# All S5 table rounds ahead of the quads, two quads' loads ahead for the second half, and the gelu and z stores issued by ScalarE

## The chip, the core and the metric

The kernel runs on one core of a Trainium2 chip. The metric is the device time of one execution in microseconds; the figure for the kernel before is the median of three runs, and one further execution was profiled. Engine names as in the profile: PE is TensorE, DVE is VectorE, ACT is ScalarE, POOL is GpSimd, SP is SyncE, which does no arithmetic here and issues every DMA of the kernel before. Each engine takes its own instructions strictly in the order in which they stand in its program.

## What is computed

One inference step of a hybrid decoder layer, all in float32, for a prompt of 2048 tokens and 8 single-token samples (2056 columns). The parts that matter here:

```
proj = rmsnorm(x) @ w_in              # 1024 -> 512 columns u (S5) + 512 columns v (pooling)
# S5 head: 32 groups x 16 channels, 64 complex states per group
h    = scan over time of (a_bar * h + b_bar u)
y    = gelu(Re(C h) + D u);   y = y * sigmoid(y @ w_glu)
# pooling head: 4 channel groups, windows 2/4/8/16
z    = (windowed mean(v) - v) @ pool_w * pool_scale
x    = x + concat(y, z) @ w_out
x    = x + w_down(gelu(conv(w_up rmsnorm(x)))...)   # gated FFN, 2 x 2816 wide
```

The FFN takes some 1400 of the 2000 us and is not touched by the change. What it touches is the mixer in front of it.

## The kernel before, in words

**Tiles and halves.** The columns are cut into five `SUBS` (512, 512, 512, 264 and 256 columns) and, from the gate on, into eight `CSUBS` of about 256. Time is also cut into two halves of 1024 tokens, since the S5 state of the second half starts from the end of the first. Weights are [128 x 128] blocks. Each float32 operand is split into a high and a low part (a cast on ACT, a subtraction on DVE or POOL: `split`, lines 75 and 76), and a product is three matmuls (`mm3`, lines 87 to 89).

**The input projection.** `units(half, ms, subs)` runs one `unit` for each column tile and each of eight blocks `m` of 128 outputs. For m = 0 to 3 the result is a piece of u: it is scaled by DVE (line 733) and stored to `u_d`. For m = 4 to 7 it is a piece of v: `pool_path` takes the windowed sums (DVE lines 657, 662, 673; POOL line 665 `wsum`) and `pool_z` multiplies by `pool_w` (PE line 697 into `ps_z`), lets ACT scale the result into `zt` (line 699; two buffers) and stores it to `z_d` in one or two DMAs (line 703). `prep_x` loads and splits the next column tile of x (`xraw`, `xh` on ACT line 79, `xl` on DVE line 80).

**The S5 part in the background.** The 32 groups are eight quads of four groups. Pieces of S5 work wait in the list `bg`; `back()` takes the next one after each unit and gives it a priority that lies 50 steps (`BGO`) behind the units, so that a scheduler lays it between them when engines are free. The pieces are:
- `rot(r)`, r = 0 to 3: a round that builds a quarter of the rotation table by doublings, 20 DVE instructions on `rt` with the scratch tile `ra` (`level`, lines 279, 280, 282), a copy and a negation on ACT (lines 290 and 295), and four stores to `tab_d[r]` by SP (lines 298 and 299). `rt` shares the two buffers of the tag `tab` with the quads' own tables, and `ra` shares the single buffer of the tag `yg` with the gelu's result.
- `s5_build(q)`: operators of quad q, mostly on POOL, with eight small DMAs `ops<-kt` (line 539).
- `s5_load(half, q)`: loads `U`, the operators (second half only) and `tab` (lines 552 to 566).
- `s5_scan(half, q)`: four matmuls into `psw` (line 585), the rotation and the scan on DVE (lines 600 to 613), the result `H` (line 619). `psw` has one buffer.
- `s5_out(half, q)`: eight matmuls into `psy` (lines 637 and 638), gelu on ACT into `yg` (line 639), and a store to `y_d` by SP (line 640).

The list for the first half is build 0, rot 0, build 1, rot 1, then for each quad: load, (for the first two quads) the next round, scan of the quad before, out of the quad before that. So rounds 2 and 3 stand between the loads and the first two scans.

**The transition.** When the list is empty, `s5_queue(1)` puts the second half's 24 pieces in it, and `units(1, (6, 7), [2])` and, after the load of `w_glu` (`wgr`, split into `wg0` to `wg3`) and of y (`y_load`, which needs all four `y_d[m]` of the first half), `units(1, (6, 7), [3, 4])` finish the projection. Then `gate_in` multiplies y by `w_glu` (`ps_g`), loads z back (`zr`), and `out_proj` multiplies with `w_out` (`wo0` to `wo7`, loaded through two raw buffers by `res_w`, line 859) into `ps_o`, calling `back()` once for each of the eight row blocks d. All of `bg` has to be done before the gate of column tile 4 (`s5_end`).

**DMA completion.** Each DMA signals on one of eight semaphores in rotation, whichever engine issues it, so an issue also waits until the DMA eight places before it has landed.

Of the kernel before, what the change touches and what calls it, by code (L numbers as in the profile page):

```python
# [40 lines left out]
BGO = 50  # L41
# [3 lines left out]
def build(tc, a):  # L45
    nc = tc.nc
    V, S, P, T, Y = nc.vector, nc.scalar, nc.gpsimd, nc.tensor, nc.sync
    es = ExitStack()
    with es:
# [3 lines left out]
        y_d = [[dram.tile([8, 128, 128], F32, name=f"y_d{m}_{h}") for h in range(2)] for m in range(4)]  # L53
# [121 lines left out]
        with ExitStack() as er_:  # L175
# [108 lines left out]
            def rot(r):  # L284


                cs = slice(4 * r, 4 * r + 4)
                tab = sp.tile([128, 2, 4, 128], F32, tag="tab", name="rt", bufs=2)
                ta = sp.tile([128, 2, 4, 64], F32, tag="yg", name="ra")
                S.copy(out=tab[:, :, :, 0:8], in_=pwr["tab0"][:, :, cs])  # L290
                for lv in range(3, 7):
                    n = 1 << lv
                    level(tab, ta[:, :, :, 0:n], lv, cs, tab[:, :, :, 0:n], tab[:, :, :, n:2 * n])
                neg = ta.rearrange("p x g c -> p (x g c)").rearrange("p (g c) -> p g c", c=128)
                S.mul(out=neg, in_=tab[:, 1], mul=-1.0)
                for gl in range(2):
                    gp = slice(gl * 64, gl * 64 + 64)
                    Y.dma_start(out=tab_d[r][:, 0:2, :, gl], in_=tab[gp].rearrange("n x (q e) c -> n x q e c", e=2))
                    Y.dma_start(out=tab_d[r][:, 2, :, gl], in_=neg[gp].rearrange("n (q e) c -> n q e c", e=2))
# [328 lines left out]
            def s5_out(half, qd):  # L628
                U, ops, tab, H = lds.pop((half, qd))
                m, r0 = qd // 2, (qd % 2) * 64  # L630
                n = 128 if half == 0 else 136
                o = 136 - n
                yg = sp.tile([128, 4, 136], F32, tag="yg", name="yg", bufs=1)
                yps = psW.tile([128, 4, 256], F32, tag="Yp", name="psy")
                for i in range(4):
                    yo = yps[:, i, 0:n]
                    T.matmul(yo, lhsT=ops[:, i, 128:256], rhs=U[:, i, o:136], start=True, stop=False)
                    T.matmul(yo, lhsT=ops[:, i, 272:400], rhs=H[:, i, o:136], start=False, stop=True)
                S.activation(out=yg[:, :, 0:n], in_=yps[:, :, 0:n], func=AF.Gelu)
                Y.dma_start(out=y_d[m][half][:, r0:r0 + 64].rearrange("t (h g) c -> t h g c", h=16), in_=yg[:, :, n - 128:n])  # L640
                if half == 1:
                    Y.dma_start(out=ys_d[m][r0:r0 + 64].rearrange("(h g) n -> h g n", h=16), in_=yg[0:16, :, 0:8])

# [50 lines left out]
            def pool_z(i, m, pl):  # L694
                t0, n = SUBS[i]
                pz = psA.tile([128, 512], F32, tag="mm", name="ps_z")
                T.matmul(pz[:, :n], lhsT=pw_[:, m, :], rhs=pl[:, :n], start=True, stop=True)
                zt = vp.tile([128, 512], F32, tag="zt", name="zt", bufs=2)
                S.activation(out=zt[:, :n], in_=pz[:, :n], func=AF.Copy, scale=col(C_PS, m))
                o = 0  # L700
                for c in PARTS[i]:
                    w = CSUBS[c][1]
                    Y.dma_start(out=z_d[c][m], in_=zt[:, o:o + w])
                    o += w

            uts = {}
# [36 lines left out]
            def flush():  # L743
                todo, later[:] = later[:], []
                for f in todo:
                    f()
# [16 lines left out]
            bg = []  # L763
# [5 lines left out]
                    bg.pop(0)()  # L769
                    tc.cur_priority = p  # L770

            def s5_queue(half):
                out = []
                for q in range(10):
                    if q < 8:
                        out.append(lambda q=q: s5_load(half, q))
                    if 1 <= q < 9:
                        out.append(lambda q=q - 1: s5_scan(half, q))
                    if 2 <= q:
                        out.append(lambda q=q - 2: s5_out(half, q))  # L780
                return out
# [12 lines left out]
            bg.append(lambda: s5_build(0))  # L794
            bg.append(lambda: rot(0))
            bg.append(lambda: s5_build(1))
            bg.append(lambda: rot(1))
            for q in range(10):
                if q < 8:
                    bg.append(lambda q=q: (q > 1 and s5_build(q), s5_load(0, q)))  # L800
                if q < 2:
                    bg.append(lambda q=q: rot(q + 2))
                if 1 <= q < 9:
                    bg.append(lambda q=q - 1: s5_scan(0, q))
                if 2 <= q:
                    bg.append(lambda q=q - 2: s5_out(0, q))
# [10 lines left out]
                units(1, (m,))  # L817
            while bg:
                back()
            bg.extend(s5_queue(1))  # L820
            units(1, (6, 7), [2])
            epar.close()
            exa.close()
# [7 lines left out]
                wg.append(lambda k, hi=hi, lo=lo: (hi[:, k, :], lo[:, k, :]))  # L831
            y0 = y_load(ce, 0)
            units(1, (6, 7), [3, 4])
            flush()

        def s5_end():
# [13 lines left out]
        if True:  # L850
# [53 lines left out]
            def out_proj(i, g, nxt):  # L904
                t0, n = CSUBS[i]
                acc = ct("acc", bufs=2)
                x1 = cx.tile([128, KT, CW], F32, tag="x1", name="x1", bufs=2)
                for d in range(KT):
                    xt = ct("xt", bufs=2)
                    Y.dma_start(out=xt[:, :n], in_=a["xT"][d, :, t0:t0 + n])  # L910
                    ps = ps_c("ps_o")
                    mm3(ps[:, :n], lambda k: wo[d]((k + 4) % 8), g)
                    V.tensor_tensor(out=x1[:, d, :n], in0=ps[:, :n], in1=xt[:, :n], op=ALU.add)
                    if d == 0:
                        S.activation(out=acc[:, :n], in_=x1[:, d, :n], func=AF.Square)
                    else:
                        sq = ct("sq", bufs=1)
                        S.activation(out=sq[:, :n], in_=x1[:, d, :n], func=AF.Square)  # L918
                        P.tensor_tensor(out=acc[:, :n], in0=acc[:, :n], in1=sq[:, :n], op=ALU.add)  # L919
                    if True:  # L920
                        back()
                    if d == 0:
                        for f in pend:
                            f()
                        pend.clear()
                    if d == 4:
                        nxt()
                    if i == len(CSUBS) - 1 and d % 2:
                        Y.dma_start(out=x1_d[i][:, d - 1:d + 1], in_=x1[:, d - 1:d + 1, :n])
                if i == len(CSUBS) - 1:  # L930
                    rstd_from([acc[:, :n]], rs_last, n)
                else:
                    pend.append(lambda: norm_out(i, x1, acc))
# [299 lines left out]
        with ExitStack() as ed:  # L1233
# [114 lines left out]
            for name, wop, bop in steps:  # L1348
                W = {}
                for i, (t0, n, n2) in enumerate(UNITS):  # L1350
                    if i == 0:
                        W[0], r = first if name == "p1" else (weights(wop, 0), acts(bop, 0))
                    else:
                        r = acts(bop, i)
# [120 lines left out]
```

## Time and profile before

| what | us |
|---|---|
| median of three runs | 2013.78 (2013.4 to 2015.46) |
| the profiled execution | 2005.36 |
| its span, first to last instruction | 2003.6 |
| PE busy | 1871.8 (93%) |
| DVE busy | 1424.5 (71%) |
| ACT busy | 894.9 (45%) |
| POOL busy | 908.2 (45%) |

The stages in the span: the input projection with the first half's S5 to about 303 us, the transition to about 375, out_proj with the second half's S5 to about 600, FFN up to about 1510, FFN down to the end. A timeline row is one instruction, or several alike in a row, with its start, its duration, engine, line, operation, output <- inputs, shape, a count (`x8`), and in brackets the idle time of that engine just before it and the instruction that ended the idle time. The records of some float32 matmuls come in pairs (`x2` for one matmul, `x8` for four).

### The profile page before, as it was taken

The numbers are of one execution on the slowest core, as the hardware profiler recorded it, in microseconds if no ns is written. First come the engines' busy times: TensorE is split into PE (matmuls) and PEld (weight loads), VectorE is DVE, ScalarE is ACT, GpSimd is POOL, SyncE is SP. The second block draws the span as 40 slices with busy tenths as digits, with TensorE's granted clock in tenths as the row PEclk, the third lists the DMA queues.
The fourth block names the chain that finished last, engine by engine and source line by source line (L and its number), as shares of the span: only waits on it lengthen the run. The fifth ranks groups of instructions, "written<-read, shape, count | busy, mean of one in ns | idle before, by whom it ended". The sixth has DMA issues, their size and how long they took to land.

```text
span 2003.6 us, 38367 instructions
## 1 busy us (share of the span) xinstructions
PE 1871.8 (93%) x14680; PEld 1810.5 (90%) x14680; DVE 1424.5 (71%) x2423; ACT 894.9 (45%) x1665; POOL 908.2 (45%) x1091
## 2 busy tenths in 40 slices
PE   6886985899998999999997999999998999999998
PEld 4666874899997999999997999999998999999997
DVE  8887776686568878777789877787876335354675
ACT  5332223444444555555555555555554323323332
POOL 4363672211136445454547555554541066135751
PEclk9998996999998999999998999999998999999999
DMA  6564657775554333333334323332326485347763
GB/s 218 165 178 120 199 139 208 188 218 152 145 168 143 115 118 125 106 90 100 103 107 129 122 87 105 98 110 89 107 81 236 152 277 171 102 162 222 239 207 120
DMA packets 214216, 296.62 MB, mean 148 GB/s; under 512 B 41216, under 2 KB 157824, under 8 KB 213776
## 3 DMA queue, kind: packets, MB, share of 16 engines
q1 hardware_dynamic: 214032, 294.17, 46.8%
q8 instruction: 115, 1.88, 0.4%
q14 instruction: 69, 0.57, 0.1%
HBM read 199.60 MB, written 93.32 MB: 146 GB/s over the span
## 4 chain that ended last, share of the span: by engine, by line
PE 54%; POOL 4%; DMA 3%; DVE 3%; issue 3%; ACT 1%; DVEq 0%; SPq 0%; POOLq 0%; ACTq 0%
PE ps_X L1140 8%; PE ps_X L1139 8%; PE ps_X L1138 8%; PE ps_Z L1139 4%; PE ps_Z L1140 4%; PE ps_Z L1138 4%; PE ps_d L88 4%; PE ps_d L87 4%; PE ps_d L89 4%; PE ps_Y L1140 2%; PE ps_Y L1138 2%; PE ps_Y L1139 2%; DMA wr<-w_dn 1%; POOL xo L1300 1%; DMA x_d<-xo 1%
## 5 line engine op out<-in xcount | busy, mean ns | idle before, releaser
L87 PE MATMUL ps_d<-bh,wh 128*128 128x256 f32 (+1 forms) x1232 | 343.7, 283 | 11.1 <-ACT bh L75 11.1
L88 PE MATMUL ps_d<-bl,wh 128*128 128x256 f32 (+1 forms) x1232 | 347.1, 283 | 3.8 <-DVE bl L76 3.6
L89 PE MATMUL ps_d<-bh,wl 128*128 128x256 f32 (+1 forms) x1232 | 346.4, 282 | 0.0
L76 DVE TENSOR_TENSOR wl<-raw,wh 128x512 fp32r<-128x512 f32 x308 | 274.8, 895 | 59.0 <-ACT wh L75 54.8
L1166 DVE SCALAR_TENSOR_TENSOR ps_cv<-hup,cst,ps_cv 128x512 f32<-128x512 f32 x352 | 258.1, 750 | 53.8 <-ACT ps_cv L1164 51.4
L75 ACT CAST wh<-raw 128x512 fp32r<-128x512 f32 x308 | 189.8, 620 | 232.1 <-PE ps_X L1139 164.0
L1073 POOL TENSOR_TENSOR raw<-raw 128x512 f32<-128x512 f32 x176 | 243.7, 1386 | 83.0 <-DVE wl L76 69.5
L87 PEld LDWEIGHTS ps_d<-bh,wh 128*128 128x128 f32 x1232 | 230.8, 189 | 12.0 <-ACT bh L75 12.0
L88 PEld LDWEIGHTS ps_d<-bl,wh 128*128 128x128 f32 x1232 | 232.3, 189 | 4.9 <-DVE bl L76 4.9
L89 PEld LDWEIGHTS ps_d<-bh,wl 128*128 128x128 f32 x1232 | 232.8, 189 | 0.0
L76 DVE TENSOR_TENSOR bl<-br,bh 128x1536 fp32r<-128x1536 f32 (+3 forms) x56 | 113.7, 2032 | 99.2 <-ACT bh L75 95.3
L1164 ACT ACTIVATE ps_cv<-hup,cst 128x512 f32<-128x512 f32 x176 | 135.9, 782 | 7.7 <-DVE hup L1126 3.7
L87 PE MATMUL ps_in<-xh,wh 128*128 128x512 f32 (+2 forms) x288 | 109.2, 379 | 8.3 <-ACT xh L79 7.4
L919 POOL TENSOR_TENSOR acc<-acc,sq 128x256 f32<-128x256 f32 (+1 forms) x56 | 45.0, 804 | 154.2 <-ACT sq L918 148.9
L88 PE MATMUL ps_in<-xl,wh 128*128 128x512 f32 (+2 forms) x288 | 104.2, 362 | 4.5 <-DVE xl L80 4.5
L1093 POOL TENSOR_TENSOR tt<-cv 128x256 f32<-128x256 f32 (+1 forms) x88 | 78.9, 906 | 64.5 <-DVE cv L1173 29.5
L75 ACT CAST bh<-br 128x1536 fp32r<-128x1536 f32 (+3 forms) x56 | 76.6, 1376 | 63.5 <-PE ps_d L89 60.6
L89 PE MATMUL ps_in<-xh,wl 128*128 128x512 f32 (+2 forms) x288 | 103.8, 361 | 1.0 <-DVE wl L76 0.9
L1138 PE MATMUL ps_X<-bt2h,wh 128*128 128x256 f32 (+1 forms) x352 | 100.2, 285 | 2.5 <-ACT p L1121 2.5
L1140 PE MATMUL ps_X<-b11h,wl 128*128 128x256 f32 (+1 forms) x352 | 99.4, 282 | 3.1 <-DVE wl L76 3.1
L1139 PE MATMUL ps_Y<-b21l,wh 128*128 128x256 f32 (+1 forms) x352 | 99.7, 284 | 2.5 <-DVE b21l L76 2.5
L1139 PE MATMUL ps_X<-b11l,wh 128*128 128x256 f32 (+1 forms) x352 | 99.4, 282 | 2.2 <-DVE b11l L76 2.2
(436 smaller groups left out, 6497.0 us busy)
## 6 DMA issues: line engine op xcount, KB each, us to landing
raw<-w_up SPq DMA_DIRECT2D x176, 256.0 KB, 2.7
wr<-w_dn SPq DMA_DIRECT2D x36, 704.0 KB, 4.2
op_d<-tt SPq DMA_DIRECT2D x33, 512.0 KB, 3.1
br<-op_d SPq DMA_DIRECT2D x21, 768.0 KB, 5.3
br<-op_d SPq DMA_DIRECT2D x21, 640.0 KB, 3.9
op_d<-cv SPq DMA_DIRECT2D x33, 256.0 KB, 2.7
wr<-w_in SPq DMA_DIRECT2D x16, 512.0 KB, 5.1
tab<-tab_d SPq DMA_DIRECT2D x32, 256.0 KB, 6.6
```

What stands on the lines that cost most here:

```text
L75: S.copy(out=hi, in_=src)
L76: (eng or V).tensor_tensor(out=lo, in0=src, in1=hi.bitcast(F32), op=ALU.subtract)
L87: T.matmul(ps, lhsT=wh, rhs=rh, start=k == 0, stop=False)
L88: T.matmul(ps, lhsT=wh, rhs=rl, start=False, stop=False)
L89: T.matmul(ps, lhsT=wl, rhs=rh, start=False, stop=k == K - 1)
L1073: P.tensor_tensor(out=r, in0=x, in1=y, op=op)
L1093: P.tensor_tensor(out=o, in0=x, in1=y, op=ALU.subtract)
L1138: T.matmul(ps, lhsT=wh[:, k], rhs=hh[:, k], start=first and k == 0, stop=False, skip_group_check=not first)
L1139: T.matmul(ps, lhsT=wh[:, k], rhs=hl[:, k], start=False, stop=False, skip_group_check=not first)
L1140: T.matmul(ps, lhsT=wl[:, k], rhs=hh[:, k], start=False, stop=k == 3, skip_group_check=not first)
L1164: S.activation(out=c, in_=h[:, o:o + 512], func=AF.Identity, scale=tap(2, jj), bias=col(C_CB, jj))
L1166: V.scalar_tensor_tensor(out=c, in0=h[:, o - 2 + k:o + 510 + k], scalar=tap(k, jj), in1=c, op0=ALU.mult, op1=ALU.add)
```

## The change

It has four edits. (1) The stores of the gelu's result (`y_d`, 16 DMAs) and of z (`z_d`, 32 DMAs) are issued by ACT instead of SP. (2) The rounds `rot(1)` to `rot(3)` all stand in the list before the first quad. (3) Of the second half's pieces only the loads of quads 0 and 1 are issued ahead, before `units(1, (6, 7), [2])` (`s5_ahead`); the other 22 pieces enter the list only after the last units, where before six pieces (loads 0 to 2, scans 0 and 1, out 0) were taken between those units. (4) `out_proj` of column tile 0 calls `back()` twice for each d.

```diff
-                Y.dma_start(out=y_d[m][half][:, r0:r0 + 64].rearrange("t (h g) c -> t h g c", h=16), in_=yg[:, :, n - 128:n])
+                S.dma_start(out=y_d[m][half][:, r0:r0 + 64].rearrange("t (h g) c -> t h g c", h=16), in_=yg[:, :, n - 128:n])
...
-                    Y.dma_start(out=z_d[c][m], in_=zt[:, o:o + w])
+                    S.dma_start(out=z_d[c][m], in_=zt[:, o:o + w])
...
-            def s5_queue(half):
+            def s5_ahead(half):
+                p = tc.cur_priority
+                tc.cur_priority = p + BGO
+                s5_load(half, 0)
+                s5_load(half, 1)
+                tc.cur_priority = p
+
+            def s5_queue(half, n0):
                 out = []
                 for q in range(10):
-                    if q < 8:
+                    if n0 <= q < 8:
                         out.append(lambda q=q: s5_load(half, q))
...
             bg.append(lambda: s5_build(1))
-            bg.append(lambda: rot(1))
+            for r in range(1, 4):
+                bg.append(lambda r=r: rot(r))
             for q in range(10):
                 if q < 8:
                     bg.append(lambda q=q: (q > 1 and s5_build(q), s5_load(0, q)))
-                if q < 2:
-                    bg.append(lambda q=q: rot(q + 2))
...
-            bg.extend(s5_queue(1))
+            s5_ahead(1)
             units(1, (6, 7), [2])
...
             units(1, (6, 7), [3, 4])
+            bg.extend(s5_queue(1, 2))
             flush()
...
-                    if True:
+                    for _ in range(1 if i else 2):
                         back()
```

**Place 1: round 3 and the first two quads, DVE.** Before, DVE has this after `H` of quad 0 (`t_1661` and `t_1668` are quad 0's scratch, `t_1841` is quad 1's; L279 to L282 are the round):

```order
L619 TENSOR_TENSOR H<-psw,t_1668 128x4x128
L279 TENSOR_TENSOR ra<-rt,ns 128x4x8 x2
L280 TENSOR_TENSOR rt<-rt,nc 128x8x8
L282 TENSOR_TENSOR rt<-rt,ra 128x4x8 x2
L279 TENSOR_TENSOR ra<-rt,ns 128x4x16 x2
L280 TENSOR_TENSOR rt<-rt,nc 128x8x16
L282 TENSOR_TENSOR rt<-rt,ra 128x4x16 x2
L279 TENSOR_TENSOR ra<-rt,ns 128x4x32 x2
L280 TENSOR_TENSOR rt<-rt,nc 128x8x32
L282 TENSOR_TENSOR rt<-rt,ra 128x4x32 x2
L600 TENSOR_TENSOR t_1841<-psw,tab 64x512
```

After the change the same place reads:

```order
L619 TENSOR_TENSOR H<-psw,t_1668 128x4x128
L600 TENSOR_TENSOR t_1841<-psw,tab 64x512
L601 TENSOR_TENSOR t_1841<-psw,tab 64x512
L602 TENSOR_TENSOR psw<-psw,tab 128x512
L608 TENSOR_TENSOR psw<-psw,t_1841 128x512
L613 SCALAR_TENSOR_TENSOR psw<-dec,psw 128x512
```

Quad 1's scan now follows quad 0's result directly; the round's last level, which stood among quad 1's rows before, is gone from there too.

**Place 2: where round 3 stands now, DVE.** Among the pooling of the first columns and the splits of the third column tile (`vt`, `csum`, `pl` are the pooling, `xl` the split of x):

```order
L657 TENSOR_TENSOR vt<-ps_in,rstd 128x512
L279 TENSOR_TENSOR ra<-rt,ns 128x4x8 x2
L662 SCALAR_TENSOR_TENSOR csum<-ones,vt 128x528
L282 TENSOR_TENSOR rt<-rt,ra 128x4x8 x2
L279 TENSOR_TENSOR ra<-rt,ns 128x4x16 x2
L280 TENSOR_TENSOR rt<-rt,nc 128x8x16
L80 SCALAR_TENSOR_TENSOR xl<-xraw,cst,xh 128x512
L282 TENSOR_TENSOR rt<-rt,ra 128x4x16 x2
L80 SCALAR_TENSOR_TENSOR xl<-xraw,cst,xh 128x512
L673 SCALAR_TENSOR_TENSOR pl<-wsum,vt 128x512
L279 TENSOR_TENSOR ra<-rt,ns 128x4x32 x2
L280 TENSOR_TENSOR rt<-rt,nc 128x8x32
```

Before, `vt`, `csum`, `xl` and `pl` stood here without the round's rows between them; the round has moved in front of the first quad's scan and into this block.

**Place 3: the end of the projection, ACT and POOL.** Before, ACT has around the gelu of quad 7 of the first half (the second `yg` row is not shown; `wg3h` and `yh` wait for loads):

```order
L699 ACTIVATE zt<-ps_z,cst 128x264
L75 CAST wg3h<-wgr 128x512
L75 CAST yh<-yr 128x256
L639 ACTIVATE yg<-psy 128x4x128
L606 COPY bus<-psw 128x32
```

and after the change:

```order
L639 ACTIVATE yg<-psy 128x4x128
L699 ACTIVATE zt<-ps_z,cst 128x256
L640 DMA y_d_0_75<-yg 8x64x128
L703 DMA z_d_88<-zt 128x256
L75 CAST wg3h<-wgr 128x512
L606 COPY bus<-psw 128x32
L699 ACTIVATE zt<-ps_z,cst 128x256
L703 DMA z_d_88<-zt 128x256
L75 CAST yh<-yr 128x256
```

The gelu and a z tile have moved ahead of the two casts, and their stores stand on ACT behind them. POOL had the low part of `wg3` in front of the last two window sums:

```order
L76 TENSOR_TENSOR wg3l<-wgr,wg3h 128x512
L623 COPY H<-hs 128x4x8
L624 COPY H<-hcar 128x4
L665 TENSOR_TENSOR wsum<-csum 128x256
L625 COPY hcar<-H 128x4
```

and now has it behind them:

```order
L665 TENSOR_TENSOR wsum<-csum 128x256
L625 COPY hcar<-H 128x4
L658 COPY vcar<-vt 128x16
L665 TENSOR_TENSOR wsum<-csum 128x256
L554 MEMSET U 128x4x8
L555 MEMSET U 128x4x8
L76 TENSOR_TENSOR wg3l<-wgr,wg3h 128x512
```

So the last window sums no longer stand behind the split of `wg3`.

## Rows read from the trace of the kernel before

**Rows 1.** Windows: length; PE, PEld, DVE, ACT, POOL busy; granted clock, DMA share, GB/s.
```profile
125.00:150.00 25.00, 21.23 (x89) 15.60 (x90) 23.26 (x36) 11.55 (x18) 15.91 (x13) 1.00 0.82 236
150.00:175.00 25.00, 22.23 (x133) 19.87 (x131) 18.38 (x34) 8.31 (x18) 5.20 (x6) 0.86 0.45 130
175.00:200.00 25.00, 12.30 (x70) 10.65 (x71) 21.32 (x37) 6.46 (x10) 12.01 (x12) 0.83 0.42 109
...
300.00:325.00 25.00, 13.14 (x65) 10.79 (x64) 13.43 (x30) 4.47 (x9) 4.92 (x17) 0.72 0.81 229
325.00:350.00 25.00, 15.04 (x75) 13.51 (x75) 17.43 (x30) 12.81 (x24) 6.32 (x7) 0.64 0.59 191
...
400.00:600.00 200.00, 197.57 (x1646) 195.89 (x1645) 137.66 (x317) 92.51 (x196) 46.76 (x67) 1.00 0.59 172
sum 500.00, PE 442.24 PEld 407.51 DVE 354.48 ACT 186.81 POOL 189.11; mean PE 40.20 PEld 37.05 DVE 32.23 ACT 16.98 POOL 17.19
```

**Rows 2.** Timeline of PE, 154 to 198 us.
```profile
154.30 0.59 PE L122 MATMUL ps_rb<-rs_d,ones 128*128 128x8 f32 x2 [2.73 <-DVE rs_d L121]
...
176.77 1.13 PE L585 MATMUL psw<-U,ops 128*128 128x128 f32 x8 [1.81 <-ACT rt L290]
...
177.86 0.38 PE L637 MATMUL psy<-U,ops 128*128 128x128 f32 x2
...
197.50 0.79 PE L637 MATMUL psy<-U,ops 128*128 128x128 f32 x2 [10.93 <-ACT yg L639]
```

**Rows 3.** Timeline of ACT, 190 to 198 us.
```profile
190.39 0.63 ACT L295 ACTIVATE ra<-rt 128x512 f32<-128x512 f32 x1 [9.73 <-DVE rt L282]
...
195.56 1.28 ACT L639 ACT_TABLE_LOAD   x1 [2.68 <-DMA tab_d<-ra]
196.85 0.60 ACT L639 ACTIVATE yg<-psy 128x512 f32<-128x512 f32 x1
```

**Rows 4.** Timeline of DVE, 186 to 197 us, quad 1's scan.
```profile
186.24 0.69 DVE L600 TENSOR_TENSOR t<-psw,tab 64x512 f32<-64x512 f32 x1
...
195.80 0.69 DVE L619 TENSOR_TENSOR H<-psw,t 128x512 f32<-128x512 f32 x1
```

**Rows 5.** Windows of rounds 2 and 3, instructions on `rt` alone: DVE, ACT.
```profile
113.00:126.00 13.00, 8.60 (x20) 0.87 (x2) 1.00 0.46 137
176.00:192.00 16.00, 11.57 (x20) 0.85 (x2) 0.99 0.19 54
```

**Rows 6.** Timeline of PE, 308 to 350 us, the five longest waits.
```profile
308.20 1.22 PE L697 MATMUL ps_z<-pl,pw__287 128*128 128x256 f32 x2 [4.17 <-DVE pl L687]
...
313.30 2.15 PE L585 MATMUL psw<-U,opsl 128*128 128x136 f32 x8 [2.01 <-DMA z_d<-zt]
...
323.04 0.58 PE L87 MATMUL ps_g<-yh,wg1h 128*128 128x256 f32 x1 [4.81 <-ACT zt L699]
...
334.89 0.56 PE L637 MATMUL psy<-U,opsl 128*128 128x136 f32 x1 [3.53 <-ACT yg L639]
...
349.37 0.58 PE L89 MATMUL ps_o<-gh,wo2l 128*128 128x256 f32 x1 [4.76 <-DVE wo2l L76]
```

**Rows 7.** Timeline of POOL and ACT around the split of `wg3`.
```profile
304.77 1.26 POOL L76 TENSOR_TENSOR wg3l<-wgr,wg3h 128x512 fp32r<-128x512 f32 x1 [4.19 <-ACT wg3h L75]
...
304.08 0.62 ACT L75 CAST wg3h<-wgr 128x512 fp32r<-128x512 f32 x1 [4.97 <-DMA wgr<-w_glu]
...
308.47 0.59 ACT L639 ACTIVATE yg<-psy 128x512 f32<-128x512 f32 x1
```

**Rows 8.** Timeline of SP's DMA issues, 292 to 326 us.
```profile
292.40 5.32 SPq L539 DMA_DIRECT2D ops<-kt  x8
...
314.03 0.64 SPq L640 DMA_DIRECT2D y_d<-yg  x1
...
319.05 0.38 SPq L149 DMA_DIRECT2D yr<-y_d  x1
...
325.22 0.58 SPq L859 DMA_DIRECT2D wo0r<-w_out  x1
```

## The prediction

> **What bounds the kernel now.** I read the page's slices first: PE is near full but for a few dents, so time can be won only where PE stands still or runs at its lower clock. The windows show where that is in the part that the change touches [rows 1]: from 400 to 600 us PE is busy 197.57 of 200 us, while it has 12.30 us of 25 in the window from 175 and 13.14 and 15.04 us in the two from 300, at a granted clock of 0.72 and 0.64 there. So two places matter, and what lies behind 400 us is PE's own work.
>
> The first place is one wait: PE stands 10.93 us before the `psy` matmul of quad 1, until 197.50 [rows 2]. The row names the gelu of quad 0 on ACT. ACT is late because its table load stood until 195.56 behind a DMA, the store of round 3's scratch `ra` [rows 3]: gelu output and `ra` share one buffer. The round itself stands between quad 0's `H` and the end of quad 1's scan, so that scan, too, ran only from 186.24 to 196.49 [rows 4]. Two chains thus end at the same time, and both are held by round 3.
>
> The second place is the transition. Five waits of 4.17, 2.01, 4.81, 3.53 and 4.76 us make 19.3 us [rows 6]. The first is for a window sum which stood on POOL behind `wg3l`, which had waited 4.19 us for the cast of `wg3` [rows 7]. That cast also stood in front of the last gelu (308.47) on ACT; its store was issued by SP only at 314.03, and the load of that y at 319.05 [rows 7, 8].
>
> **The change, part by part.**
>
> *Round 3 out of the two quads.* Without the round, ACT can take quad 0's gelu as soon as its `psy` is done, and nothing of the wait for `ra` is left. What is late next is quad 1's `H`. Its scan took 196.49 − 186.24 = 10.25 us [rows 4], at the longest, since the round's last level stood among its rows. It can start when `psw` of quad 1 is done, at 176.77 + 1.13 = 177.9 [rows 2], and would end by 188.2, while PE comes to the wait at 197.50 − 10.93 = 186.6. So at least 9.3 us of the wait can go, and all of it if the last level took over 1.6 us, which 5 of the round's 20 instructions in 11.57 us [rows 5] make likely. I take the whole; as a lower bound 8, if DVE, busy 21.32 of 25 us there [rows 1], puts other work between. Behind the wait a pair of `psy` matmuls took 0.79 us where it took 0.38 before it [rows 2]: the lower of the two clock levels. I count 1 us for that. Sum: −12, between −8 and −13.
>
> *Round 3 in its new place.* It costs DVE 11.57 us where it was and 8.60 us for round 2 [rows 5]. The new place is the pooling of the first columns, about 130 to 145 us, just behind round 2; I take 8.6. DVE is busy 23.26 of 25 us there and 18.38 of the next 25 [rows 1], so 8.4 us are free in 50. Were all of it usable, the round would cost nothing; were none, 8.6 to 11.6 us. PE already waits for DVE there (2.73 us at 154.30 [rows 2]), and DVE's idle time is broken into pieces in which it waits for loads of x, which themselves wait for DVE to free a buffer. So I let a third be used: 8.6 − 2.8 = about +6, between 0 and +12. SP's four stores of the round now stand among those loads and wait for the round's end; that is why I don't take less.
>
> *The stores on ACT.* 48 issues leave SP. No row shows an issue on ACT; the nearest is SP's 0.64 us for a y store [rows 8]. At most 48 × 0.64 = 31 us are put on ACT, which is busy 186.81 of the 500 us from 100 to 600 [rows 1], so the time itself is covered by idle time. The waits in front of these issues are not: behind each stand ACT's casts, z tiles and gelus, and DVE and PE wait for those. This I take as 0 and price in a rival. What SP gains shows in the transition: the y store was issued 314.03 − 309.06 = 4.97 us after the gelu's end [rows 7, 8]; from ACT it goes out behind one z tile.
>
> *The transition.* With the gelu and the last z tiles in front of the `wg3` cast on ACT, and both window sums in front of `wg3l` on POOL, the 4.17 us of the first wait go. The y store and so the load of y come about 5 us earlier, and with them the matmuls that need all of y. The third wait was for a z tile that came late on ACT; the z tiles stand ahead now, and what is late next is y, whose 5 us I have counted, so I don't count it again. The waits at 334.89 and 349.37 lie behind `wo0r`, issued at 325.22 [rows 8], since the table loads in front of it on SP wait for quad 0's scan, as they still do after the change. They move with the front and don't shrink. Sum: −9. The lower bound is −2, if the scan of quad 0 stays the last to come; the upper −18, about two thirds of what is at stake: 19.3 us of waits and, at clocks of 0.72 and 0.64, 13.14 × 0.28 + 15.04 × 0.36 = 9 us of slow matmuls [rows 1, 6].
>
> The Trainium skill has a rule that speaks against this part. "DMA: Bandwidth & Descriptors", section "Issuing engines are not separate DMA queues", says that issuing from several engines saves only the sequencer's time to issue, usually small beside the transfer. By it the y store of quad 7 and the six z stores of the last column tiles would give back 7 × 0.64 = 4.5 us at most in place of 9, and the sum would be −10.5; no row here can show it yet, but the 4.97 us above are a wait in SP's order and not issue time.
>
> *The second half's queue.* Scans 0 and 1 leave the last units, but on PE they stay at nearly the same place among the `ps_g`; 17 of the 22 remaining pieces then run in the first `out_proj`. DVE is busy 137.66 of 200 us from 400 on, PE 197.57 [rows 1], so a denser chain of scans fits on average; I take 0, with up to +4 for PE waiting for `H` in the first column tile.
>
> Sum: −12 + 6 − 9 + 0 = −15 us, so 1990 us against the profiled execution's 2005.36. That execution lies 8.4 us under the median of 2013.78; the difference carried over gives 1999 us.
>
> **The rivals.**
>
> *The round is only moved, not hidden (about 2009 us).* DVE and the loads of x pass on nearly all of the round, +10, and in the transition quad 0's scan is still what everything waits for, −2 to −3: −12 + 10 − 3 = −5. For it: DVE is at 93% in the new place. Against it: 6.6 us of DVE are free in the window after it [rows 1].
>
> *ACT waits for SP's DMAs (about 2020 us, slower).* Each issue waits until the DMA eight places before it has landed, and for z stores these are often the small `ops<-kt` stores of SP, a group of which takes 5.32 us to issue [rows 8]. When SP is late, ACT now stands in front of its casts of x, and its z tiles hold PSUM buffers that the projection needs. If four of the eight quads' groups cost PE a whole group each, that is 4 × 5.32 = 21 us, and −15 + 21 = +6. It decides as soon as a z tile becomes ready while the group before it is still being issued. Against it: before the change the same stores stood in the same rotation on SP, between the same groups, and PE's windows there were not marked by it.
>
> *The transition opens up (about 1989 us).* If the loads of x hide the round (+1) and half of the 28 us at stake in the transition goes, −12 + 1 − 14 = −25. For it: nearly all its waits hang on one chain from `wg3` through y to `wo0`; against it: the loads of `w_out` are serial through two buffers.
>
> That the round is not moved at all is excluded by the order of the instructions.
>
> **How the numbers follow.** I give the forecast 0.50, the moved round 0.22, ACT's waits 0.14, the open transition 0.14. A measurement of this kernel can tell about 0.2%, 4 us, from no change. The forecast (its own range 1990 to 2007) and the open transition are faster, 0.64, and of the moved round (−5) a bit over half, 0.12: 0.76. Within 0.2% is the rest of the moved round, 0.10; slower is ACT's waits, 0.14. Predicted is the forecast's 1999; the range from 1987 to 2018 reaches into both outer cases and leaves out less than 0.2.
>
> **What would show it.** Right: no wait over 3 us on PE before `psy` of quad 1; DVE's rows of round 3 at 130 to 145 us and PE's waits there longer by some 6 us; the window sums right behind their `csum` on POOL; the y store on ACT within 2 us of the gelu, and the first `ps_o` some 9 us earlier than the front that enters the transition. Wrong: ACT's issue rows with idle time of several us before them, named by `ops<-kt`, and PE waiting for `xh` or `zt` behind them; or a first `out_proj` in which PE stands at `psy` for `H` by more than 4 us in sum.

## The result and the profile after

The changed kernel takes **1994.88 us** (median; 1989.31 to 1998.54) against 2014.62 us for the kernel before in the same runs: a ratio of 0.9899, 95% interval [0.9872, 0.9927]. That is 20 us less, between 15 and 26. The forecast was 1999 us, 15 less.

The two profiled executions are only 8 us apart (spans 2003.6 and 1995.5 us), since the one of before lies some 9 us under its kernel's median and was quicker in the FFN, which the change does not touch. I therefore compare the traces at the entrance of the FFN: PE's wait for `rs_d` in front of the first FFN matmuls. Timeline rows of PE, first of before, then of after: the first z matmul behind the first two quads, the first `ps_g`, the first `ps_o`, the first sum of squares in `out_proj` (`ps_st`), the last `psy` of the second half, the FFN's entrance.

```profile
231.14 1.02 PE L697 MATMUL ps_z<-pl,pw__287 128*128 128x512 f32 x2
316.12 0.58 PE L87 MATMUL ps_g<-yh,wg0h 128*128 128x256 f32 x1 [0.21 <-ACT zt L699]
339.31 0.41 PE L87 MATMUL ps_o<-gh,wo0h 128*128 128x256 f32 x1
398.69 0.28 PE L133 MATMUL ps_st<-ones,acc 128*128 128x1 f32 x2
453.69 0.40 PE L638 MATMUL psy<-H,opsl 128*128 128x136 f32 x2
603.85 1.20 PE L122 MATMUL ps_rb<-rs_d,ones 128*128 128x128 f32 x4 [4.69 <-DVE rs_d L121]
```

```profile
225.04 1.02 PE L697 MATMUL ps_z<-pl,pw__287 128*128 128x512 f32 x2
298.36 0.47 PE L87 MATMUL ps_g<-yh,wg0h 128*128 128x256 f32 x1
323.62 0.41 PE L87 MATMUL ps_o<-gh,wo0h 128*128 128x256 f32 x1
372.30 0.50 PE L133 MATMUL ps_st<-ones,acc 128*128 128x1 f32 x4
441.07 0.40 PE L638 MATMUL psy<-H,opsl 128*128 128x136 f32 x2
583.17 1.19 PE L122 MATMUL ps_rb<-rs_d,ones 128*128 128x128 f32 x4 [4.82 <-DVE rs_d L121]
```

The lead is 6.1 us at the first of these, 17.8, 15.7, 26.4, 12.6 and 20.7 us at the others: it is largest at the first sum of squares, and 5.7 us of it are given back by the entrance. The 20.7 us agree with the timed 20. Below, "entrance" is this last row, 603.85 us before.

The windows of after, in the columns of [rows 1], show the first place healed and the second in part:

```profile
125.00:150.00 25.00, 19.97 (x67) 14.96 (x68) 23.69 (x48) 11.73 (x19) 18.02 (x12) 0.80 0.72 208
150.00:175.00 25.00, 22.90 (x139) 19.67 (x138) 21.19 (x37) 9.01 (x20) 6.33 (x7) 1.00 0.59 168
175.00:200.00 25.00, 21.27 (x138) 18.96 (x137) 20.15 (x35) 7.93 (x13) 19.07 (x22) 0.93 0.63 185
...
300.00:325.00 25.00, 14.58 (x77) 13.15 (x76) 14.69 (x27) 10.84 (x22) 5.04 (x10) 0.74 0.82 244
325.00:350.00 25.00, 21.44 (x160) 20.28 (x159) 18.21 (x34) 12.05 (x22) 10.47 (x10) 0.92 0.56 182
```

From 175 us PE is busy 21.27 us where it was 12.30. From 125 us it has 1.3 us less, at a clock of 0.80 where it was 1.00: that is the price of the moved round. Of the two windows from 300 us the first is still poor, at 14.58 us and 0.74; the second went from 15.04 us at 0.64 to 21.44 at 0.92.

PE in after at the places of [rows 2] and [rows 6]: the wait that the round now makes, the first `psy` of quad 1, which no longer waits, and waits of the transition.

```profile
142.59 1.22 PE L122 MATMUL ps_rb<-rs_d,ones 128*128 128x128 f32 x4 [3.89 <-DVE rs_d L121]
...
186.55 0.38 PE L637 MATMUL psy<-U,ops 128*128 128x128 f32 x2
...
310.92 0.79 PE L638 MATMUL psy<-H,opsl 128*128 128x136 f32 x2 [3.96 <-DVE H L619]
...
318.81 0.50 PE L637 MATMUL psy<-U,opsl 128*128 128x136 f32 x2 [1.89 <-ACT yg L639]
...
328.89 0.54 PE L89 MATMUL ps_o<-gh,wo2l 128*128 128x256 f32 x1 [0.42 <-DVE wo2l L76]
```

The wait of 10.93 us is gone altogether, and that of 4.17 us for a window sum too. A wait of 3.96 us for quad 0's `H` is new; the 4.76 us for `wo2l` are down to 0.42.

ACT, POOL and SP in after, at the places of [rows 7] and [rows 8]:

```profile
297.36 0.60 ACT L639 ACTIVATE yg<-psy 128x512 f32<-128x512 f32 x1 [3.05 <-PE psy L638]
298.28 0.61 ACTq L640 DMA_DIRECT2D y_d<-yg  x1
301.75 0.62 ACT L75 CAST wg3h<-wgr 128x512 fp32r<-128x512 f32 x1 [3.06 <-DMA wgr<-w_glu]
...
296.16 0.73 POOL L665 TENSOR_TENSOR wsum<-csum 128x256 f32<-128x256 f32 x1 [0.15 <-DMA opsl<-ops_d]
302.44 1.27 POOL L76 TENSOR_TENSOR wg3l<-wgr,wg3h 128x512 fp32r<-128x512 f32 x1 [5.30 <-ACT bus L606]
...
304.98 0.38 SPq L149 DMA_DIRECT2D yr<-y_d  x1
311.39 0.58 SPq L866 DMA_DIRECT2D wo0r<-w_out  x1
```

The window sums no longer stand behind `wg3l`. The y store goes out 0.32 us after the gelu's end (4.97 before), the load of y at 304.98 (319.05 before), `wo0r` at 311.39 (325.22).

What the issues cost ACT: the view of the two store lines gives duration as minimum/median/maximum in ns.

```profile
L703 ACTq DMA_DIRECT2D z_d<-zt x32: 321/341/2363, 107.7 to 303.6; - x32
...
L640 ACTq DMA_DIRECT2D y_d<-yg x16: 583/604/1162, 183.7 to 444.7; - x16
```

By the medians 32 × 0.341 + 16 × 0.604 = 21 us of ACT's sequencer, where I had allowed 31.

### The profile page after: what moved, and what is told of

Read it like the earlier page. It is cut to its first block, busy times and chain, and to the rows that moved or that the text cites. A ratio compares the mean times of both kernels' runs of the same rounds, so it can differ in the third digit from the quotient of the medians.

```text
span 1995.5 us, 38363 instructions
## 1 busy us (share of the span) xinstructions
PE 1877.3 (94%) x14680; PEld 1815.0 (91%) x14680; DVE 1404.4 (70%) x2423; ACT 898.1 (45%) x1666; POOL 904.7 (45%) x1091
## 4 chain that ended last, share of the span: by engine, by line
PE 55%; POOL 4%; DVE 4%; DMA 3%; issue 3%; ACT 1%; DVEq 0%; POOLq 0%; ACTq 0%; SPq 0%
PE ps_X L1147 8%; PE ps_X L1146 8%; PE ps_X L1145 8%; PE ps_d L88 4%; PE ps_d L87 4%; PE ps_d L89 4%; PE ps_Z L1146 4%; PE ps_Z L1147 4%; PE ps_Z L1145 4%; PE ps_Y L1147 2%; PE ps_Y L1145 2%; PE ps_Y L1146 2%; DMA x_d<-xo 1%; DMA wr<-w_dn 1%; POOL xo L1307 1%
## 5 line engine op out<-in xcount | busy, mean ns | idle before, releaser
L76 DVE TENSOR_TENSOR wl<-raw,wh 128x512 fp32r<-128x512 f32 x308 | 270.5, 881 | 64.0 <-ACT wh L75 61.5
```

The costliest lines, as they stand in the source:

```text
L76: (eng or V).tensor_tensor(out=lo, in0=src, in1=hi.bitcast(F32), op=ALU.subtract)
```

## The experiments

The change has three parts: R, the rounds in front; S, the stores on ACT; Q, the two queue edits (loads ahead with the rest behind the units, and two pieces per block). All ratios below are to the kernel before timed on the same chip; the entrance is from one trace of each kernel.

### Each part alone

R alone:
```diff
-            bg.append(lambda: rot(1))
+            for r in range(1, 4):
+                bg.append(lambda r=r: rot(r))
...
-                if q < 2:
-                    bg.append(lambda q=q: rot(q + 2))
```


> The kernel before with the table rounds 1 to 3 queued ahead of the quads, and nothing else. Theory (the edits add up): PE's wait of 10.93 us before quad 1's psy goes, round 3 costs up to 5 us at about 140 us, and PE reaches the seventh ps_z some 6 us earlier than before (231.1 us there, so 225); the transition keeps its length, so the first long wait of the FFN edge (603.9 us before) comes at about 597 and the whole is 6 us faster. Rival (the transition is what the rounds decide, since the quads of the second half start earlier with them): the FFN edge at 590 or below.

S alone:
```diff
-                Y.dma_start(out=y_d[m][half][:, r0:r0 + 64].rearrange("t (h g) c -> t h g c", h=16), in_=yg[:, :, n - 128:n])
+                S.dma_start(out=y_d[m][half][:, r0:r0 + 64].rearrange("t (h g) c -> t h g c", h=16), in_=yg[:, :, n - 128:n])
...
-                    Y.dma_start(out=z_d[c][m], in_=zt[:, o:o + w])
+                    S.dma_start(out=z_d[c][m], in_=zt[:, o:o + w])
```

> The kernel before with the y and z stores issued by ScalarE, and nothing else. Theory: nothing changes up to 231 us (within 2 us, the 10.93 us wait stays), the transition gets 9 to 15 us shorter, the FFN edge comes at about 590 to 595. Rival (issuing from another engine saves issue time alone): at most 4.5 us, FFN edge at 599 or later. Rival (ScalarE waits in order for SyncE's DMAs): PE's waits for xh and zt grow by several us and the FFN edge is later than 604.

Q alone:
```diff
-            bg.extend(s5_queue(1))
+            s5_ahead(1)
...
+            bg.extend(s5_queue(1, 2))
...
-                    if True:
+                    for _ in range(1 if i else 2):
```

> The kernel before with two quads' loads ahead, the other 22 pieces after the last units and two pieces per row block in the first out_proj, and nothing else. Theory: the first place stays as before (10.93 us wait), the transition gains up to 5 us, since the two window sums need not wait behind the split of wg3, and some 5 us are given back in out_proj, where PE waits for H; FFN edge within 3 us of 603.9. Rival (the queue carries the gain in the transition): FFN edge at 595 or below.

| kernel | ratio [95%] | entrance | against 603.9 |
|---|---|---|---|
| R | 1.0002 [0.9987, 1.0017] | 602.4 | −1.5 |
| S | 0.9996 [0.9980, 1.0011] | 604.7 | +0.8 |
| Q | 0.9954 [0.9936, 0.9971] | 595.5 | −8.3 |

My theories for R (6 us faster) and S (9 to 15) failed; for Q the rival came, all but half a us. R alone brings nothing, and yet the wait of 10.93 us is gone in its trace and its z matmul that stands at 231.14 us before stands at 222.6: 8.5 us ahead. It still leads by as much in the second column tile of `out_proj` and has lost all but 1.5 us at the entrance. S alone leads by 12.3 us in that tile and loses it, too. So a lead at the transition is not yet a gain: it can be lost again in `out_proj`. S alone shows the place where; the rows of ACT and PE there:

```profile
467.04 0.62 ACT L75 CAST yh<-yr 128x256 fp32r<-128x256 f32 x1 [6.29 <-DMA yr<-y_d]
```

```profile
469.31 1.01 PE L133 MATMUL ps_st<-ones,acc 128*128 128x1 f32 x4 [4.91 <-POOL acc L919]
```

ACT stands 6.29 us in order at the cast of a `yr`, the y of column tile 4, the first of the second half, whose load needs that half's last y store; the squares for `acc` stand behind it, and PE waits for `acc`. In S, R and before the last `psy` is nearly at the same time (452.7, 451.4 and 453.7 us), so the last quad comes no earlier, and S, which arrives early, waits for it. R shows it in part only: between the second and the third sum of squares, where its lead goes from 8.5 to 2.9 us, PE stands for 2.5 us and works 3.2 us longer.

### Two parts together

RQ is the changed kernel with the diff of S turned back, SQ the changed kernel with that of R turned back, RS the changed kernel with the old queue and one piece per block:
```diff
-            s5_ahead(1)
+            bg.extend(s5_queue(1, 0))
...
-            bg.extend(s5_queue(1, 2))
...
-                    for _ in range(1 if i else 2):
+                    for _ in range(1):
```

> The changed kernel with its y and z stores issued by SyncE again, so rounds and queue without the stores. Alone, the rounds gave 0 and the queue gave 8 us (0.46%). Theory (the queue lets the 8 to 9 us lead that the rounds alone had at 430 us survive): 14 to 18 us faster than before, FFN edge at 586 to 591. Rival (the lead of the rounds is lost in any case behind the transition): 7 to 10 us faster, FFN edge at about 595.

> The changed kernel with the old order of the table rounds, so stores and queue without the rounds. Theory (the stores need the queue: with the casts and window sums out of the way, the y store is issued at once): the 10 us wait near 197 us stays, the transition up to the first ps_o is as short as in the changed kernel, about 14 us faster than before, FFN edge at about 590. Rival (the stores give nothing in any company, as alone): 7 to 10 us faster, FFN edge at about 595.

> The changed kernel with the old queue of the second half (six pieces between the last units, one piece per row block), so rounds and stores without the queue. Theory (the queue is what makes room): 0 to 6 us faster than before, with a wait of over 4 us in the transition as in each edit alone. Rival (any two edits add up to more than each alone): 10 us faster or more, FFN edge below 594.

| kernel | ratio [95%] | entrance | the part it lacks is worth, added last |
|---|---|---|---|
| RQ | 0.9916 [0.9899, 0.9933] | 586.7 | S: −3.5 |
| SQ | 0.9935 [0.9919, 0.9951] | 588.9 | R: −5.7 |
| RS | 0.9947 [0.9929, 0.9965] | 592.4 | Q: −9.2 |
| RSQ (the change) | 0.9899 [0.9872, 0.9927] | 583.2 | |

My theories came true for RQ and SQ; for RS the rival came (two edits give more than each alone). The parts are not additive: alone −1.5, +0.8 and −8.3 make −9.0, together they make −20.7. The queue carries most, by itself and added last. The interval of the change overlaps those of RQ and SQ, so by the times alone S and R, added last, cannot be told from nothing; their 3.5 and 5.7 us rest on one trace each.

What the queue does at the first `out_proj` is seen on DVE, where `wo0l` and `wo2l` stand among quad rows. Rows of DVE, before and then after:

```profile
332.36 1.23 DVE L76 TENSOR_TENSOR wo0l<-wo0r,wo0h 128x1024 fp32r<-128x1024 f32 x1 [7.52 <-ACT wo0h L75]
...
344.25 0.69 DVE L600 TENSOR_TENSOR t<-psw,tab 64x512 f32<-64x512 f32 x1
...
348.09 1.23 DVE L76 TENSOR_TENSOR wo2l<-wo2r,wo2h 128x1024 fp32r<-128x1024 f32 x1
```

```profile
318.18 1.23 DVE L76 TENSOR_TENSOR wo0l<-wo0r,wo0h 128x1024 fp32r<-128x1024 f32 x1 [6.90 <-ACT wo0h L75]
...
326.17 0.70 DVE L608 TENSOR_TENSOR psw<-psw,t 128x512 f32<-128x512 f32 x1
327.61 1.22 DVE L76 TENSOR_TENSOR wo2l<-wo2r,wo2h 128x1024 fp32r<-128x1024 f32 x1
```

Before, `wo2l` came 15.7 us after `wo0l`, behind a quad's multiplications by the table and its scans; after, 9.4 us behind, in front of the scans. This goes with Q in every kernel: 11.6 us in Q, 11.5 in RQ, 9.6 in SQ, but 15.6 in R, 13.6 in S and 19.2 in RS.

The queue's gain lies behind the first `ps_o` and not in front of it. RS, without the queue, has its first `ps_o` at 319.49 us, 4.1 earlier than the change; its first sum of squares comes at 377.90, 5.6 later, and its entrance 9.2 later.

### Two pieces per block, taken away and added

In the changed kernel:
```diff
-                    for _ in range(1 if i else 2):
+                    for _ in range(1):
```
and in R, with the old queue:
```diff
-                    if True:
+                    for _ in range(1 if i else 2):
```

> The changed kernel with one piece per row block in the first out_proj instead of two. After the first out_proj the changed kernel gives back 6 us of a lead of 26. Theory (the dense queue of scans costs this): the lead at the first norm of out_proj stays above 24 us, and the whole is 0 to 5 us faster than the changed kernel. Rival (the later pieces only move the same work behind, and the last quad's scan ends too late for tile 4's gate): the same time within 2 us, or slower.

> The kernel before with the rounds ahead and two pieces per row block in the first out_proj, with the old queue and SyncE's stores. The rounds alone were 8 us ahead at 430 us and lost it; their last psy matmul came at 451.4, as before (453.7), and tile 4's y load needs what follows it. Theory (the end of the second half's quads decides what of a lead is kept): the last psy comes at 443 or earlier and the FFN edge at 590 to 596, 7 to 12 us faster than before. Rival (the loss has to do with ScalarE's and SyncE's order at that place and not with the quads' end): FFN edge at 600 or later, within 4 us of before.

Without the double pieces the changed kernel has a ratio of 0.9939 [0.9918, 0.9959] and the entrance at 595.3 us, 12.1 later; its last `psy` comes at 456.84 us instead of 441.07, and `wo2l` 11.7 us after `wo0l`. My theory, that it would be up to 5 us faster, was wrong, and the rival's "slower" came. Up to the first sum of squares the two kernels are level (372.25 and 372.30 us); the loss lies behind, and the last quads come late, as the rival had it. Added to R, the double pieces do nothing (0.9996 [0.9981, 1.0012], entrance 604.0). My expectation that this would bring the last `psy` to 443 us or earlier failed; it stayed at 452.13, so this run could not test whether an early last `psy` frees R's lead. It showed the same wait in the same place:

```profile
468.73 1.01 PE L133 MATMUL ps_st<-ones,acc 128*128 128x1 f32 x4 [5.11 <-POOL acc L918]
```

So that the last quad's y holds the lead back is read from these waits and from times that go together: with the last `psy` at 451 us or later, R, S, R with double pieces and the kernel before have their entrance at 602 to 605 us; Q, RQ, SQ, RS and the change, with it at 436 to 449 us, at 583 to 596. No run moved it alone, and two kernels do not fit: the changed kernel without double pieces has 456.84 and 595.3 us, the one with rounds 2 and 3 late (below) 451.23 and 593.5. This stays open.

### Where round 3 costs its time

The scratch `ra` shares its buffer with the gelu's result. To take that chain away and leave the round where it was, the gelu's results of the first two quads were given another tile's buffer, in the kernel before:
```diff
-                yg = sp.tile([128, 4, 136], F32, tag="yg", name="yg", bufs=1)
+                yg = sp.tile([128, 4, 136], F32, tag="M1" if half == 0 and qd < 2 else "yg", name="yg", bufs=1)
```

> The kernel before with the gelu results of quads 0 and 1 of the first half in another buffer than round 3's scratch, so that quad 0's gelu need not wait for the round's stores; the round stays where it was on DVE. Theory (two chains end at the same time): the gelu runs at about 181 us, but PE then waits for H of quad 1, which still ends at about 196.5, so the wait of 10.93 us shrinks by 1 us at most. Rival (the shared buffer alone): the wait falls to 2 us or less.

One execution, 2012.84 us, entrance 606.6. PE no longer waits for the gelu but stands as long nearby:

```profile
195.43 2.05 PE L585 MATMUL psw<-U,ops 128*128 128x128 f32 x8 [7.36 <-issue]
```

DVE in that kernel has rows of the round in front of and within quad 1's scan, whose `H` (row below) ends at 195.3, just before PE's row:

```profile
189.09 1.06 DVE L282 TENSOR_TENSOR rt<-rt,ra 128x256 f32<-128x256 f32 x2
...
194.64 0.69 DVE L619 TENSOR_TENSOR H<-psw,t 128x512 f32<-128x512 f32 x1
```

The next `ps_rb` comes at 200.26 us, 2.1 earlier than before (202.34). So both chains were there, as in my theory, and freeing one of them brings little.

Could the rounds stand later, between other quads? Rounds 2 and 3 before the loads of quads 3 and 5, and round 3 alone before that of quad 4, in the changed kernel (only the added lines; the loop in front keeps the other rounds):
```diff
+                if q in {3: 2, 5: 3}:
+                    bg.append(lambda q=q: rot({3: 2, 5: 3}[q]))
...
+                if q in {4: 3}:
+                    bg.append(lambda q=q: rot({4: 3}[q]))
```

> The changed kernel with round 2 queued before the load of quad 3 and round 3 before the load of quad 5, where their tables are first needed by quads 4 and 6. VectorE has 40% idle there (200 to 275 us). Theory (the cost of a round is VectorE time at a place where it is full): PE's extra 4 to 5 us at 140 us go, nothing comes in their place, FFN edge at 578 to 581, 2 to 5 us faster than the changed kernel. Rival (the round's shared buffer is what costs, wherever it stands between two quads): a wait of 4 to 10 us for a gelu or an H at 200 to 260 us, slower than the changed kernel.

> The changed kernel with only round 3 queued late, before the load of quad 4. Theory: PE's extra 4 to 5 us at 140 us go, FFN edge at 578 to 581. Rival (shared buffer): one wait of 4 to 10 us for a gelu or an H at 200 to 240 us, FFN edge at 583 or later.

Both theories failed. The kernels lose 10.3 and 17.3 us at the entrance against the changed kernel (593.5 and 600.4; ratios 0.9959 [0.9944, 0.9974] and 0.9983 [0.9973, 0.9992]). PE's longest waits there, of the first and then of the second:

```profile
161.80 2.04 PE L585 MATMUL psw<-U,ops 128*128 128x128 f32 x8 [4.21 <-DVE H L619]
185.22 0.59 PE L122 MATMUL ps_rb<-rs_d,ones 128*128 128x8 f32 x2 [5.45 <-DVE rs_d L121]
251.94 0.46 PE L585 MATMUL psw<-U,ops 128*128 128x128 f32 x2 [3.66 <-DMA U<-u_d]
```

```profile
190.59 0.76 PE L585 MATMUL psw<-U,ops 128*128 128x128 f32 x2 [5.36 <-DMA U<-u_d]
214.84 0.79 PE L87 MATMUL ps_in<-xh,wh 128*128 128x512 f32 x1 [5.30 <-DVE ut L733]
```

On DVE the late rounds stand at 176 to 189 and 222 to 234 us in the first kernel and at 204 to 216 in the second. The waits at 185.22 and 214.84 us lie inside a round, for DVE's `rs_d` and for a piece of u; the ones at 161.80 and 190.59 come ahead of any late round, so they have another cause, which was not looked for. So in the places tried a round between quads made the kernel slower than one in front of the first quad, but not all of the loss is shown to be the round's own time on DVE.

### Which of the stores

RQ and the change differ by both kinds of stores. With y on ACT and z back on SP:
```diff
-                    S.dma_start(out=z_d[c][m], in_=zt[:, o:o + w])
+                    Y.dma_start(out=z_d[c][m], in_=zt[:, o:o + w])
```

> The changed kernel with the z stores back on SP; only the y stores stay on ACT. With both kinds on SP the gate edge of the FFN (PE's wait for rs_d at line 122) lay at 586.7 us, with both on ACT at 583.2. Theory (what the stores give is the y store's earlier issue at the end of the first half): the edge stays at 583 to 584.5 us, the ratio at 0.988 to 0.991, and the last gelu's y store is issued within 2 us of the gelu. Rival 1 (the z stores carry it: six z stores of the last column tiles no longer stand on SP in front of the loads of y and w_out): the edge comes at 586 to 588 us and the ratio at 0.991 to 0.993. Rival 2 (mixing is the worst of all, since SP's z stores wait for zt in front of the loads of y while the semaphore rotation now also ties them to ACT's): later than 588 us.

Only the second rival's time came: a ratio of 0.9996 [0.9985, 1.0006] and the entrance at 602.1 us, 19.0 us later than the change and 15.4 later than with both kinds on SP. Rows of ACT:

```profile
297.69 0.60 ACT L639 ACTIVATE yg<-psy 128x512 f32<-128x512 f32 x1 [4.96 <-PE psy L638]
303.98 0.60 ACTq L640 DMA_DIRECT2D y_d<-yg  x1
304.62 0.62 ACT L75 CAST wg3h<-wgr 128x512 fp32r<-128x512 f32 x1 [6.34 <-DMA tab<-tab_d]
```

The gelu ends at 298.29, 0.33 us later than in the change; its store is issued 5.69 us behind it, and the trace names the load of a table that SP had issued: the DMA eight places before the store. With the issue itself ACT does nothing else for 6.34 us, and behind it stand the cast of `wg3` and a z tile; PE then waits for `zt`:

```profile
306.34 0.58 PE L87 MATMUL ps_g<-yh,wg0h 128*128 128x256 f32 x1 [4.61 <-ACT zt L699]
```

Yet against RQ, where SP issues this store, nothing was lost up to here. RQ's y store comes at 304.08 us, its load of that y at 308.74, its first `ps_g` at 306.75 and its first `ps_o` at 326.28; with y on ACT these are 303.98, 308.68, 306.34 and 326.74. So the engine that issues the y store made no difference to when it goes out. The loss against RQ is 8.5 us at the first sum of squares (391.25 against 382.72) and 15.4 at the entrance; the last `psy` is 20 us later (456.29 against 435.88). It was not traced to one wait, so the price of ACT's standing still stays open.

The kernel before has the same wait on SP. Rows of SP up to its y store at 314.03 [rows 8], which is the eighth DMA behind the first of the two table loads:

```profile
306.23 1.26 SPq L566 DMA_DIRECT2D tab<-tab_d  x2
307.59 1.51 SPq L703 DMA_DIRECT2D z_d<-zt  x2
309.14 0.50 SPq L681 DMA_DIRECT2D out_np_p<-vt  x1
309.74 0.45 SPq L691 DMA_DIRECT2D out_np_s<-so  x1
310.29 0.42 SPq L552 DMA_DIRECT2D U<-u_d  x1
313.23 0.56 SPq L557 DMA_DIRECT2D U<-us_d  x1
```

What the store waited for by the view of SP's waits (us in total, times, longest):

```profile
SPq L640 <- DMA tab<-tab_d: 0.2, 1, 0.2
```

It is as short as 0.2 us only because SP stood 2.5 us at the DMA in front, for a load of operators.

In every kernel here with the z stores on SP, eight places before this y store stands a table load, and the store goes out 2.95 to 5.69 us behind its gelu (before 4.97, R 3.00, Q 3.08, RQ 2.95), whichever engine issues it. In every kernel with the z stores on ACT it is a load of operators or of U, and the delay is 0.03 to 2.38 us (S 0.77, SQ 2.38, RS 0.03, the change 0.32). What shortened it is the order of the DMAs and not the engine.

No kernel here was measured faster than the change.

## Why the prediction was right, step by step

- **Round 3 out of the quads (−12) and in its new place (+6): the mechanism was right; that the sum fits is in part luck.** In after PE's z matmul after the moved round comes at 148.19 us against 142.78, and `ps_rb` at 151.83 against 146.25: +5.4 and +5.6. At the next `ps_rb`, where PE waited 2.73 us before (154.30) and now does not (157.1), only +2.8 is left of it. From there to the `ps_rb` behind quad 1 (202.34 and 191.72) 13.4 us are won. That makes −10.6; some 4.5 us of it are lost again by the z matmul at 231.14 us, where the balance is −6.1, as the sum had it. PE's matmul time up to there grew from 116.7 us (from 90 us on) to 120.3, so part of the 4.5 us may be work done earlier. That two chains were held by the round was right, by the run with a buffer of its own for the gelu. What I did not see is that this gain alone would not reach the end: R alone gains nothing that can be measured. The sum treated the steps as independent, and they are not.
- **The stores on ACT (0): right for the transition; the reason for the earlier y store was wrong.** The longest that ACT stands before an issue in the transition of after is 2.4 us (a z store at 301.27), and only one z tile waited for a store, for 2.2 us. But an issue can hold ACT for 6.34 us, as in the last run. The step that failed is that the 4.97 us "are a wait in SP's order": the store stood until the table load eight places before it had landed, and by the last run it would have stood as long on ACT.
- **The transition (−9): right at its front, too small behind it.** The two gains at its front came: the window sum's wait of 4.17 us is gone, and the y store comes 4.65 us sooner after the gelu, if for the other reason. From the z matmul at 231 us to the first `ps_o` the lead grew from 6.1 to 15.7 us, by 9.6; I had said some 9. The second step that failed is "They move with the front and don't shrink", of the waits for `yg` (3.53 us) and for `wo2l` (4.76). They are 1.89 and 0.42 us now, 6.0 us less. For `wo0r` the reading was right: it still comes behind quad 0's scan, 13.8 us earlier. But `wo2l` also stood on DVE behind quad 1's scan, which the queue edit moves behind it: I looked at when the loads are issued, not at what is queued in front of the split.
- **The rule of the Trainium skill** ("DMA: Bandwidth & Descriptors", section "Issuing engines are not separate DMA queues"), that issuing from several engines saves only issue time. The trace agrees with it where the engine alone was changed: the y store and its load came within 0.1 us on either engine. By it the stores were worth 4.5 us at most and the sum −10.5. Added last, the stores are worth 3.5 us at the entrance, which this fits better than the 5 us that I put on the earlier y store. But it does not give what the edit is worth: added to R the stores are worth 10.0 us (602.4 to 592.4), alone nothing, and the y stores without the z stores cost 15 us, while their 16 issues take 16 × 0.604 = 9.7 us of a sequencer in all. What also moves is the order of the DMAs, and which engine stands still while an issue waits for an earlier one.
- **The second half's queue (0, up to +4): the term that was mis-sized.** The cost was there, 4.1 us at the first `ps_o` against RS, with a wait of 3.96 us for `H`. What the sum lacked is the gain behind it: added last, the queue brings the entrance 9.2 us earlier, and without its double pieces 12.1 us of the 20.7 are lost.
- **The rivals.** The moved round cost 5.4 us at its place and 2.8 at the next `ps_rb`, between the +1 of the open transition and the forecast's +6, and not the +10 of its own rival. The open transition's 14 us fit the net only by two errors that cancel: from the z matmul to the first sum of squares in `out_proj` 20.3 us were won (26.4 − 6.1), and 5.7 were given back by the entrance, which no term had. −6.1 − 20.3 + 5.7 = −20.7, between that rival's −25 and the forecast's −15. PE's idle time from the transition (70 us behind the z matmul) to the first sum of squares went from 27.9 to 15.9 us, at a granted clock of 0.79 and then 0.87. Where the 5.7 us go was not traced.

## What to carry to other kernels

Time won in one stage can be lost in a later one that waits for background work; alone, two of the three parts here were worth nothing, and added to the other two they were worth 3.5 and 5.7 us by one trace each. When a wait is said to move with the front, look at what stands in front of the awaited instruction on its own engine, not only at when its data are loaded. When an issue is late, look at the DMA eight places before it in the rotation: moving the issue to another engine does not shorten that wait, it moves the standing still to that engine, and each edit of the DMA order changes which DMA it is.

## What the runs showed of the hardware that I had not expected

- An issue of a store takes 341 ns (z) or 604 ns (y) of ACT in the median of after, but one that waited for a DMA of another engine held ACT for 6.34 us.
- A wait of PE can cost more than its own length: in after, after the wait of 3.89 us that ends at 142.59, the granted clock is 0.50, the lower of the two levels, up to 148.0 us and 0.99 in the 4 us behind. In the kernel before 1.64 us of waiting at that `ps_rb` were followed by a clock of 1.00.
- One traced execution of the FFN, which was not changed, can differ by some 12 us from another: the lead is 20.7 us at its entrance and 8.1 at the end of the span, while the medians differ by 20.
